# Hybrid encoder layer on one core: the softmax sums spread by DMA, operand transposes in three steps, gate rows woven into a projection

## The chip, the cores and the metric

The kernel runs on one core of a Trainium2 chip. The metric is the device time of one execution in microseconds (us). Before the change it is 1793.68 us, the median of three runs (1793.61 to 1795.17).

The engines are named as in the profile: PE is TensorE (matmuls and transposes; PEld is its weight load, which overlaps), DVE is VectorE, ACT is ScalarE, POOL is GpSimd and SP is the queue that issues the DMAs. Each engine works through its own list of instructions in a fixed order, so an instruction that waits holds up all that stand behind it.

## The reference

One layer (DEPTH is 1) over two sequences, a prompt of 512 tokens and a sample of 2048, each with 16 learned meta tokens in front. D_MODEL is 1024, all in fp32. A projection feeds two head groups; their outputs go through one output projection back into the residual.

```python
def hybrid_layer(h, norm_g, w_in, b_gate, conv_w, mlstm_norm_g, q_norm_g, k_norm_g, rpb, w_out):
    xn = rms_norm(h, norm_g)
    proj = xn @ w_in                                  # 4112 + 512 columns
    q_m, k_m, v_m, o_m, z_m, gates, q_a, k_a, v_a, z_a = jnp.split(proj, cuts, axis=-1)
    qk_m = jax.nn.silu(centred_dwconv(jnp.concatenate([q_m, k_m], axis=-1), conv_w))
    ...
    h_m = mlstm_bidir(heads_m(q_m), heads_m(k_m), heads_m(v_m), gates)   # scans in chunks
    y_m = rms_norm(sigmoid(o_m) * h_m, ...) * silu(z_m)
    qa, ka, va = rms_norm(heads_a(q_a), q_norm_g), rms_norm(heads_a(k_a), k_norm_g), heads_a(v_a)
    y_a = neighbourhood_attention(qa, ka, va, rpb) * silu(z_a)
    return h + jnp.concatenate([y_m, y_a], axis=-1) @ w_out

# neighbourhood_attention: 8 heads of 64; tokens lie on a grid 64 wide; a query sees a window of
# 8 x 16 tokens with a learned bias, and the 16 meta tokens
p = softmax(concat([q . k * scale + bias, q . k_meta * scale]))
out = p_window @ v + p_meta @ v_meta
```

The mLSTM gates give, per direction, cumulative sums and running maxima over each chunk of 128 tokens and from chunk to chunk. These are the "gate rows".

## The kernel before

**Stages.** The sample's first 1280 tokens and the meta tokens are normalised and transposed to the first set of blocks (h1). `phase_a1` projects them to q, k, v of the attention and to the gates, `phase_a1_z` to the attention's gate path z, `phase_a2` to the columns of the mLSTM. Then the same is done for the second set (h2: the rest of the sample, and the prompt): `phase_a1` (its groups 0 to 5), `phase_a1_z`, `phase_a2`. The mLSTM chunks and the output projection come last. Each projection is three matmul passes per weight tile (L239: high and low parts of an fp32 split), into tiles `mmt` (128 tokens x 256 columns) or `mmf` (128 columns x up to 512 tokens).

**Attention beside the projections.** Attention runs in pairs of heads, 8 pairs (two windows of rows) beside the end of the first set and `phase_a1` of the second, 12 pairs (three windows) beside `phase_a1_z` and `phase_a2` of the second. A generator yields after each step, and `weave(main, (att, 0.6), ...)` advances it by so many steps per step of the projection. A pair has four blocks of 128 queries. `scores(b)` makes two `sps` tiles on PE, which DVE reduces to a maximum (L863) and ACT exponentiates with the row sums in `sums` (L864). `probs(b)` transposes the result (`pps`, L876), copied to `pt` by ACT (L880) and DVE (L882). `values(half)` multiplies by v into `py` (L901). `prep(0)` transposes the queries (`qps`, L833), `prep(1)` the keys, eight transposes (`kps`, L839). `out()` takes 1/sum (L911), has POOL spread it over 64 columns (`rx`, L913), PE transpose that four times (`rb`, L916), and DVE multiply z by it (L918) and by `py` (L919).

**Gate rows.** `R.gate_rows(tp)` runs between the second `phase_a1` and the second `phase_a1_z`, after `drain(att)`. It uses buffers of the attention pool (`gmisc` in tag kt, `gbig` in tag vt). Per direction it is a chain through PE (`gps`, `gpr`, `gpc`, `gpt`, `gpd`), DVE scans and small ACT functions.

**What sets the order.** A scheduler places instructions, but the matmuls that go through `turn()` (projections, `sps`, `pps`, `py`, `qps`, `kps`) are tied on PE to the order in which the code emits them. The gate rows and `rb` are not. All DMAs go through SP. PSUM pools have two buffers each: `ps_mm` for the projections, `ps_a` for `sps`, `ps_b` for `pps`, `kps` and the mLSTM's small products, `ps_c` for `qps`, `py`, `rb` and the gate rows.

```python
    weave(R.phase_a2([meta] + h1, ap, free.append), (att, 0.3), (rl, 3))
    weave(R.phase_a1(blocks2, ap), (att, 0.6), (rl, 3))
    drain(att)
    R.last = False
    R.gate_rows(tp)
    zdone = set()
    att = R.attention(tp, [3, 4, 0], zdone)
    R.last = None
    weave(R.phase_a1_z(h2, ap, zdone), (att, 1.2))
```

Of the kernel before, what the change touches and what calls it, by code (L numbers as in the profile page):

```python
# [92 lines left out]
class Run:  # L93
# [4 lines left out]
    def setup(self):  # L98
# [18 lines left out]
        self.one = cp.tile([1, 128], F32, name="one")  # L117
        nc.vector.memset(self.one, 1.0)

        self.gates = cp.tile([128, 4, 21, 4], F32, name="gates")  # L120
# [20 lines left out]
        self.kqs = {"P": d("kqsP", [1024, NM + LP]), "S": d("kqsS", [1024, NM + LS])}  # L141
        self.yas = d("yas", [512, 2560])
        self.Mrow = d("Mrow", [2, 84 * 128])
        self.cbs = d("cbs", [20, 128, 4 * 129])
# [200 lines left out]
    def phase_a1(self, blocks, pool, first=None):  # L345

        nc, a = self.nc, self.a
        g0 = 0
        if first:
            g0 = 2  # L350
            for blk in blocks:
                for gi in range(2):
                    yield from self.a1_unit(pool, gi, self.A1[gi][1], first[gi], blk)
        for gi in range(g0, 6):
            c0, n = self.A1[gi]
            w = self.load_w(a["w_in"], c0, n)
            for blk in blocks() if callable(blocks) else blocks:
                yield from self.a1_unit(pool, gi, n, w, blk)

    def phase_a1_z(self, blocks, pool, done):  # L360
# [119 lines left out]
    def attention(self, pool, wins, zdone):  # L480

        todo = [AttPair(self, pool, wi, pair) for wi in wins for pair in range(4)]
        todo[0].load()
        todo[0].prep(0)
        yield
        todo[0].prep(1)
        yield
        prev = None
        for n, p in enumerate(todo):
            after = todo[n + 1] if n + 1 < len(todo) else None  # L490
            p.start()
# [12 lines left out]
            p.probs(1)  # L504
            if after:
                after.prep(0)
            if prev:
                while prev.pair not in zdone:
                    yield
                prev.out()  # L510
            yield
            p.values(0)
            p.scores(3)
            p.probs(2)
            if after:
                after.prep(1)
            yield
            prev = p
        prev.probs(3)
        yield  # L520
        yield
        prev.values(1)
        while prev.pair not in zdone:
            yield
        yield
        prev.out()


    def gate_rows(self, pool):
        nc = self.nc  # L530
        LNC = math.log(128.0 ** -0.5)
        NR = 84
        cp = self.const
        misc = pool.tile([128, 8, 128], F32, tag="kt", name="gmisc", bufs=2)
        zero, ones = misc[:NR, 0, :], misc[:NR, 1, :]
        nc.vector.memset(zero, 0.0)
        nc.vector.memset(ones, 1.0)
        self.cols = cp.tile([128, 2, 4, NR], F32, name="gcols")
        for d in range(2):
            big = pool.tile([128, 8, 128], F32, tag="vt", name=f"gbig{d}", bufs=2)  # L540
            mn, t, b, a, A, M, ws, ac = (big[:NR, i, :] for i in range(8))
            E = t
            row = misc[0:1, 2 + 3 * d:5 + 3 * d, :].rearrange("p a b -> p (a b)")[:, :4 * NR].rearrange("p (i r) -> p i r", i=4)
            col = self.gcol[:, d, :]
# [10 lines left out]
            nc.vector.tensor_tensor(out=a, in0=ps[:NR, 0:128], in1=b, op=ALU.subtract)  # L555
            nc.vector.tensor_tensor_scan(out=rv(A), data0=rv(a), data1=rv(zero), initial=-BIG, op0=ALU.max, op1=ALU.add)
            last = slice(127, 128) if d == 0 else slice(0, 1)
            bL, AL = b[:, last], A[:, last]
# [9 lines left out]
            for c0, nch in ((0, 4), (4, 16)):  # L568
# [6 lines left out]
                if d == 0:  # L575
                    nc.vector.tensor_copy(out=row[:, 2, fa:fa + 4], in_=row[:, 3, m0])
                    nc.vector.tensor_copy(out=row[:, 2, fa + 4:fb], in_=row[:, 3, fa:fb - 4])
                else:
                    nc.vector.tensor_copy(out=row[:, 2, fa:fb - 4], in_=row[:, 3, fa + 4:fb])
            pc = self.ps_c.tile([128, 512], F32, tag="c", name="gpc")  # L580
            nc.tensor.matmul(pc[:NR, 0:1], row[:, 2, :], self.one[:, 0:1], start=True, stop=True)
# [11 lines left out]
            nc.vector.tensor_scalar(out=M, in0=M, scalar1=mp, scalar2=None, op0=ALU.subtract)  # L593
            nc.sync.dma_start(out=self.Mrow[d].rearrange("(r j) -> r j", r=NR), in_=M)
            pt = self.ps_c.tile([128, 512], F32, tag="c", name="gpt")
            for i, x in enumerate((ac, ws, E)):
# [7 lines left out]
            nc.tensor.matmul(pd[:, 0:NR], self.one, drow, start=True, stop=True)  # L604
            nc.vector.tensor_copy(out=cols[:, 3, :], in_=pd[:, 0:NR])


# [154 lines left out]
    def load_wo(self, pool):  # L762
# [4 lines left out]
        for k in range(8):  # L767
            wr = pool.tile([128, 1024], F32, tag="wor", name="wor", bufs=1)
            nc.sync.dma_start(out=wr, in_=v[:, k, :])
            if k < 4:  # L770
                nc.vector.tensor_scalar(out=wr, in0=wr, scalar1=self.mg[:, k:k + 1], scalar2=None, op0=ALU.mult)
# [30 lines left out]
class AttPair:  # L802
# [9 lines left out]
    def load(self):  # L812
        nc, r, pool, nr, nk, f = self.nc, self.r, self.pool, self.nr, self.nk, self.f
        self.kt = pool.tile([128, 8, 128], F32, tag="kt", name="kt", bufs=2)
        self.vt = pool.tile([128, 8, 128], F32, tag="vt", name="vt", bufs=2)
        self.qt = pool.tile([128, 4, 128], F32, tag="qt", name="qt", bufs=2)
# [8 lines left out]
    def prep(self, part):  # L825

        nc, r, pool, nk = self.nc, self.r, self.pool, self.nk
        if part == 0:
# [6 lines left out]
            return  # L835
        for half in range(2):
            ps = r.ps_b.tile([128, 512], F32, tag="t", name="kps")
            for c in range(4):
                r.turn(nc.tensor.transpose(ps[:, c * nk:(c + 1) * nk], self.kt[:nk, half * 4 + c, :], r.ident[:nk, :nk]))  # L839
            nc.scalar.activation(out=self.K[:, half * 4 * nk:(half + 1) * 4 * nk], in_=ps[:, :4 * nk], func=AF.Copy, scale=r.gk)  # L840

    def start(self):
        pool = self.pool
        self.py = self.r.ps_c.tile([128, 512], F32, tag="c", name="py")
        self.sums = pool.tile([128, 2, 4], F32, tag="sums", name="sums", bufs=2)
        self.bias, self.pts, self.s, self.first = {}, {}, {}, True

    def scores(self, b):
        nc, r, pool, nk, n, bt = self.nc, self.r, self.pool, self.nk, 3 * self.nk, BTYPE[b]
        if bt not in self.bias:  # L850
            self.bias[bt] = pool.tile([128, 2, n], F32, tag="bias", name="bias", bufs=4)
            nc.sync.dma_start(out=self.bias[bt], in_=r.a[f"bias{self.wt}"][self.pair, bt])
# [7 lines left out]
        for hh in range(2):  # L860
            s = pool.tile([128, 384], F32, tag="s", name="s", bufs=6)
            mx = pool.tile([128, 1], F32, tag="mx", name="mx", bufs=4)
# [21 lines left out]
    def values(self, half):  # L884

        nc, r, nk, pts = self.nc, self.r, self.nk, self.pts.pop(half)
        order = ((1, 4, 0, 2, 3), (6, 3, 7, 5, 4))[half]
        for c in order:
# [8 lines left out]
            for run in runs:  # L897
# [4 lines left out]
                self.first = False  # L902

    def out(self):
        nc, r, pool = self.nc, self.r, self.pool
# [3 lines left out]
        zv = view(zt[:, :], [[8, 8], [64, 8], [1, 8]])  # L909

        nc.vector.reciprocal(out=self.sums, in_=self.sums)  # L911
        rx = pool.tile([128, 4, 2, 64], F32, tag="rx", name="rx", bufs=1)
        nc.gpsimd.tensor_scalar(out=rx, in0=view(self.sums[:, 0, 0:1], [[1, 4], [4, 2], [0, 64]]), scalar1=0.5, scalar2=None, op0=ALU.mult)  # L913
# [24 lines left out]
def drain(g):  # L938
    for _ in g:
        pass  # L940
# [3 lines left out]
def hymba(ctx, tc, a):  # L944
# [200 lines left out]
```

## Time and profile before

| | us |
|---|---|
| median of three runs | 1793.68 |
| the profiled execution | 1794.23 |
| its span, first to last instruction | 1792.5 |
| PE busy | 1693.5 (94%) |
| DVE, ACT, POOL busy | 906.5, 683.2, 405.3 |

The stages by the trace: the first blocks and their q, k, v, z until about 225 us, the first `phase_a2` with attention pairs until about 645, the second `phase_a1` until 843.4 (its attention ends near 720), the gate rows until 869, the second `phase_a1_z` and the first part of `phase_a2` with 12 attention pairs until about 1270, the rest of `phase_a2` until 1415, and the mLSTM with the output projection until the end. In the profile, a matmul's record overlaps the next one's, so the spacing of starts is what one costs.

### The profile page before, as it was taken

The numbers are of one execution on the slowest core, as the hardware profiler recorded it, in microseconds if no ns is written. First come the engines' busy times: TensorE is split into PE (matmuls) and PEld (weight loads), VectorE is DVE, ScalarE is ACT, GpSimd is POOL, SyncE is SP. The second block draws the span as 40 slices with busy tenths as digits, with TensorE's granted clock in tenths as the row PEclk, the third lists the DMA queues.
The fourth block names the chain that finished last, engine by engine and source line by source line (L and its number), as shares of the span: only waits on it lengthen the run. The fifth ranks groups of instructions, "written<-read, shape, count | busy, mean of one in ns | idle before, by whom it ended". The sixth has DMA issues, their size and how long they took to land. (4 is left out here: it accounts for less than half of the span.)

```text
span 1792.5 us, 32992 instructions
## 1 busy us (share of the span) xinstructions
PE 1693.5 (94%) x12476; PEld 1501.2 (84%) x12476; DVE 906.5 (51%) x2564; ACT 683.2 (38%) x1715; POOL 405.3 (23%) x383
## 2 busy tenths in 40 slices
PE   6999999999999989999799999999999899999899
PEld 6999988888989978998577777878888888877787
DVE  8896015253361266640334455353464378776662
ACT  5432223343342354222234445444444354543430
POOL 4021122221131231111011212211444232322210
PEclk9999999999999999999799999999999999999999
DMA  5466332333444554332454556754566666555431
GB/s 185 136 218 168 91 102 73 101 98 106 121 123 120 169 174 118 93 97 84 96 151 131 161 147 167 200 163 133 187 184 177 194 206 187 190 182 189 148 129 71
DMA packets 247166, 258.57 MB, mean 144 GB/s; under 512 B 17928, under 2 KB 204624, under 8 KB 247008
## 3 DMA queue, kind: packets, MB, share of 16 engines
q1 hardware_dynamic: 247008, 256.47, 47.7%
q8 instruction: 98, 1.61, 0.4%
q14 instruction: 60, 0.49, 0.1%
HBM read 183.05 MB, written 73.37 MB: 143 GB/s over the span
## 5 line engine op out<-in xcount | busy, mean ns | idle before, releaser
L239 PE MATMUL mmt<-wh,xah 128*128 128x256 f32 (+1 forms) x1536 | 438.9, 286 | 3.4 <-ACT mlo L260 3.4
L239 PE MATMUL mmt<-wl,xah 128*128 128x256 f32 (+1 forms) x1536 | 436.5, 284 | 1.4 <-POOL wl L230 1.4
L239 PE MATMUL mmt<-wh,xal 128*128 128x256 f32 (+1 forms) x1536 | 435.6, 284 | 0.0
L230 POOL TENSOR_TENSOR wl<-wr,wh 128x512 fp32r<-128x512 f32 (+1 forms) x184 | 247.3, 1357 | 700.0 <-ACT wh L229 691.9
L239 PEld LDWEIGHTS mmt<-wh,xah 128*128 128x128 f32 x1536 | 291.3, 190 | 4.7 <-ACT mlo L260 3.8
L239 PEld LDWEIGHTS mmt<-wl,xah 128*128 128x128 f32 x1536 | 290.8, 189 | 2.2 <-POOL wl L230 1.8
L239 PEld LDWEIGHTS mmt<-wh,xal 128*128 128x128 f32 x1536 | 292.3, 190 | 0.4 <-DVE xal L216 0.2
L387 DVE SCALAR_TENSOR_TENSOR acc<-craw,cw,acc 128x256 f32<-128x256 f32 (+2 forms) x192 | 147.1, 766 | 63.4 <-ACT acc L385 58.4
L229 ACT CAST wh<-wr 128x512 fp32r<-128x512 f32 (+1 forms) x184 | 110.1, 621 | 180.9 <-DMA wr<-in_w_in 135.1
L239 PE MATMUL mmf<-xah,wh 128*128 128x512 f32 x384 | 154.0, 401 | 3.0 <-ACT craw L431 1.5
L863 DVE CUSTOM_DVE_ANT_0 s<-sps,bias 128x384 f32<-128x384 f32 (+3 forms) x160 | 71.9, 483 | 161.7 <-PE sps L859 161.1
L239 PE MATMUL mmf<-xal,wh 128*128 128x512 f32 x384 | 152.0, 396 | 0.0
L239 PE MATMUL mmf<-xah,wl 128*128 128x512 f32 x384 | 151.6, 395 | 0.0
L239 PE MATMUL mmt<-wh,xbh 128*128 128x256 f32 (+1 forms) x384 | 112.3, 292 | 4.0 <-ACT xbh L215 2.7
L239 PE MATMUL mmt<-wl,xbh 128*128 128x256 f32 (+1 forms) x384 | 111.0, 289 | 0.0
L239 PE MATMUL mmt<-wh,xbl 128*128 128x256 f32 (+1 forms) x384 | 110.6, 288 | 0.4 <-DVE xbl L216 0.4
L864 ACT ACTIVATE s<-s,mx 128x384 f32<-128x384 f32 (+3 forms) x160 | 88.4, 555 | 22.0 <-DVE mx L863 21.4
L699 POOL TENSOR_TENSOR qw<-qw,kq 128x1024 f32<-128x1024 f32 (+1 forms) x20 | 63.4, 3168 | 131.9 <-ACT qw L698 121.8
L329 ACT COPY raw<-mmt 128x512 f32<-128x512 f32 x50 | 29.3, 585 | 159.1 <-PE mmt L239 152.3
L239 PEld LDWEIGHTS mmf<-xah,wh 128*128 128x128 f32 x384 | 72.6, 189 | 19.6 <-ACT craw L431 2.4
L373 DVE SCALAR_TENSOR_TENSOR zt<-zt,mmf 128x512 f32<-128x512 f32 (+1 forms) x24 | 14.4, 599 | 143.7 <-ACT zt L372 135.3
L239 PEld LDWEIGHTS mmf<-xah,wl 128*128 128x128 f32 x384 | 72.3, 188 | 17.2
(236 smaller groups left out, 3453.9 us busy)
## 6 DMA issues: line engine op xcount, KB each, us to landing
wr<-in_w_in SPq DMA_DIRECT2D x176, 256.0 KB
ozs<-vbuf SPq DMA_DIRECT2D x40, 256.0 KB
X<-Mrow SPq DMA_DIRECT2D x20, 512.0 KB
oz<-ozs SPq DMA_DIRECT2D x20, 512.0 KB
v<-vms SPq DMA_DIRECT2D x38, 256.0 KB
bias<-in_bias SPq DMA_DIRECT2D x24, 384.0 KB
x<-in_xs SPq DMA_DIRECT2D x16, 512.0 KB
kq<-kqsS SPq DMA_DIRECT2D x16, 512.0 KB
```

The source lines that it names most:

```text
L229: nc.scalar.copy(out=wh[:, ks, :n], in_=wr[:, :, :n])
L230: nc.gpsimd.tensor_tensor(out=wl[:, ks, :n], in0=wr[:, :, :n], in1=wh.bitcast(F32)[:, ks, :n], op=ALU.subtract)
L239: self.turn(nc.tensor.matmul(ps, st(s, k), mv(m, k), start=i == 0, stop=i == last))
L329: nc.scalar.copy(out=raw, in_=ps)
L373: nc.vector.scalar_tensor_tensor(out=t[:, :n], in0=t[:, :n], scalar=1.0, in1=ps[:, :n], op0=ALU.add, op1=ALU.mult)
L387: nc.vector.scalar_tensor_tensor(out=acc[:, :n], in0=raw[:, d:d + n], scalar=self.cw[:, ct, d:d + 1], in1=acc[:, :n], op0=ALU.mult, op1=AL ...
L699: nc.gpsimd.tensor_tensor(out=qw[:, :nd], in0=qw[:, :nd], in1=qT.unsqueeze(1).to_broadcast([128, nd, 4, 128]), op=ALU.mult)
L863: nc.vector.tensor_tensor_reduce(out=s[:, :n], in0=pss[hh][:, :n], in1=self.bias[bt][:, hh], op0=ALU.add, op1=ALU.min, scale=-1.0, scalar= ...
L864: nc.scalar.activation(out=s[:, :n], in_=s[:, :n], func=AF.Exp, scale=-1.0, bias=mx[:, 0:1], accum_out=self.sums[:, hh, b:b + 1])
```

## The change

Four things, and two smaller ones.

1. `out()` loses `rx` and the four `rb` transposes. A new step `weights()` takes 1/sum, writes it to a DRAM scratch (`rsum`, 2 x 4 x 128), and reads it back as two broadcasts over 64 partitions each into an SBUF tile `rb`. The factor 0.5 that `rx` held moves to the rows 4 to 7 of w_out in `load_wo`.
2. `prep` has three parts: queries, four key transposes, four key transposes. The key tiles go from pool `ps_b` to `ps_c`, and `py` is allocated at the first `values`, not at `start`.
3. `gate_rows` becomes a generator, on buffers of the pool `bp`. It waits until the gates are projected (`gated`) and attention has ended (`rested`), and is woven into the second `phase_a1` at 0.25 steps per step.
4. `load()` is called two pairs ahead, with three `vt` buffers. To pay for it, `bias` goes from 4 to 3 buffers and `s` from 6 to 4.

```diff
-        todo[0].load()
-        todo[0].prep(0)
-        yield
-        todo[0].prep(1)
-        yield
+        for i in range(3):
+            todo[0].prep(i)
+            yield
+        todo[1].load()
...
             p.scores(0)
             if prev:
                 prev.probs(3)
-            if after:
-                after.load()
             yield
             if prev:
                 prev.values(1)
             p.scores(1)
             p.probs(0)
+            if prev:
+                prev.weights()
+            if after:
+                after.prep(0)
             yield
             p.scores(2)
             p.probs(1)
             if after:
-                after.prep(0)
+                after.prep(1)
...
                 prev.out()
+            if n + 2 < len(todo):
+                todo[n + 2].load()
             yield
             p.values(0)
             p.scores(3)
             p.probs(2)
             if after:
-                after.prep(1)
+                after.prep(2)
...
     def gate_rows(self, pool):
+        while self.gated < 2 or not self.rested:
+            yield
...
-            if k < 4:
-                nc.vector.tensor_scalar(out=wr, in0=wr, scalar1=self.mg[:, k:k + 1], ...)
+            nc.vector.tensor_scalar(out=wr, in0=wr, scalar1=self.mg[:, k:k + 1] if k < 4 else 0.5, ...)
...
+    def weights(self):
+        nc.vector.reciprocal(out=self.sums, in_=self.sums)
+        rows = r.rsum[r.nsum % 2]
+        r.nsum += 1
+        nc.sync.dma_start(out=rows.rearrange("h b q -> q h b"), in_=self.sums)
+        self.rb = self.pool.tile([128, 512], F32, tag="rb", name="rb", bufs=1)
+        for hh in range(2):
+            nc.sync.dma_start(out=self.rb[hh * 64:hh * 64 + 64], in_=bcast(rows[hh].rearrange("b q -> (b q)"), 64))
...
-        nc.gpsimd.tensor_scalar(out=rx, ...)
-        rb = r.ps_c.tile([128, 512], F32, tag="c", name="rb")
-        for b in range(4):
-            nc.tensor.transpose(rb[:, b * 128:(b + 1) * 128], rx[:, b].rearrange("p h d -> p (h d)"), r.ident)
-        nc.vector.tensor_tensor(out=zv, in0=pv(rb), in1=zv, op=ALU.mult)
+        nc.vector.tensor_tensor(out=zv, in0=pv(self.rb), in1=zv, op=ALU.mult)
...
-    weave(R.phase_a1(blocks2, ap), (att, 0.6), (rl, 3))
+    gates = R.gate_rows(bp)
+    weave(R.phase_a1(blocks2, ap), (att, 0.6), (rl, 3), (gates, 0.25))
     drain(att)
+    drain(gates)
     R.last = False
-    R.gate_rows(tp)
```

**PE, the gate rows.** Before, both directions stand in one piece between the first column tile of z (`mmf`) and the second attention's query transposes (`qps`):

```order
L239 MATMUL mmf<-xbh,wl 128x256
L560 MATMUL gpr<-ident,gbig_9869 1x84
L561 MATMUL gpr<-ident,gbig_9869 1x84
L581 MATMUL gpc<-one,gmisc 84x1
L582 MATMUL gpc<-one,gmisc 84x1
L597 MATMUL gpt<-ident,gbig_9869 128x84 x3
L598 MATMUL gpt<-ident,gcol 1x84
L604 MATMUL gpd<-gmisc,one 128x84
L547 MATMUL gps<-ident,gates 84x128
```

Now each piece stands between projection matmuls (`mmt`) of the second `phase_a1`; this is the piece `gpt` of the first direction:

```order
L245 MATMUL mmt<-wl,xah 128x256
L245 MATMUL mmt<-wh,xal 128x256
L614 MATMUL gpt<-ident,v_8652 128x84 x2
L614 MATMUL gpt<-ident,kT 128x84
L615 MATMUL gpt<-ident,gcol 1x84
L245 MATMUL mmt<-wh,xah 128x256
L245 MATMUL mmt<-wl,xah 128x256
```

Between one piece and the next of a direction now stand 25 or more matmuls of the projection, where before there were none.

**DVE, 1/sum and its use.** These are the rows around the second pair's reciprocal in the second attention; `ISA s,mx` is the reduction of `scores`, `pt` the copy of `probs`. Before:

```order
L882 COPY pt<-pps 128x3x128
L911 RECIPROCAL sums<-sums 128x8
L373 SCALAR_TENSOR_TENSOR zt<-zt,mmf 128x256
L863 ISA s,mx<-sps,bias 128x384
L863 ISA mx 128x1
```

Now:

```order
L898 COPY pt<-pps 128x3x128
L925 RECIPROCAL sums<-sums 128x8
L940 TENSOR_TENSOR zt<-rb,zt 128x8x8x8
L381 SCALAR_TENSOR_TENSOR zt<-zt,mmf 128x512
L879 ISA s,mx<-sps,bias 128x384
L879 ISA mx 128x1
```

The multiplication by `rb` (L940), which waits for the broadcast DMAs, stands right behind the reciprocal here and ahead of the next reductions; behind the other reciprocals stand up to two blocks' reductions before it.

**SP, the new DMAs.** The same pair on SP; `rsum` is the write of 1/sum, `rb` its broadcasts, `vt`, `kt` the loads ahead:

```order
L837 DMA kt<-ks 96x8x128
L838 DMA kt<-kmeta 8x8x128
L928 DMA rsum_109<-sums 128x8x1
L931 DMA rb<-rsum_109 64x512 x2
L383 DMA zs<-zt 128x512
L868 DMA bias<-in_bias 128x768
L837 DMA vt<-vs 96x8x128
```

The broadcasts stand directly behind the write that they wait for, with z's stores, a bias table and the next loads behind them on the queue.

## Rows read from the trace of the kernel before

**Rows 1.** The page: busy times, PE and its granted clock in 40 slices
```profile
PE 1693.5 (94%) x12476; PEld 1501.2 (84%) x12476; DVE 906.5 (51%) x2564; ACT 683.2 (38%) x1715; POOL 405.3 (23%) x383
PE   6999999999999989999799999999999899999899
PEclk9999999999999999999799999999999999999999
```
**Rows 2.** Stretches: us, busy PE, PEld, DVE, ACT, POOL, granted clock, DMA share, GB/s
```profile
846.80:869.40 22.60, 6.65 (x26) 3.89 (x26) 13.31 (x58) 8.31 (x16) 3.19 (x3) 0.62 0.35 97
870.20:877.20 7.00, 7.00 (x29) 5.62 (x28) 0.75 (x1) 0.06 (x1) 0.00 (x0) 0.83 1.02 181
```
**Rows 3.** PE in order of time, 846 to 874: start, us, instruction
```profile
846.36 0.28 PE L239 MATMUL mmf<-xbl,wh 128*128 128x256 f32 x1
846.47 0.28 PE L239 MATMUL mmf<-xbh,wl 128*128 128x256 f32 x1
848.16 0.23 PE L560 MATMUL gpr<-ident,gbig 84*1 84x84 f32 x1 [1.41 <-DVE gbig L554]
...
869.42 1.11 PE L833 MATMUL qps<-ident,qt 128*128 128x128 f32 x4
```
**Rows 4.** Groups of PE from 846.8 to 869.4, costliest first: idle before, releasers
```profile
L581 PE MATMUL gpc<-one,gmisc 1*84 1x1 f32 x4 | 0.9, 282 | 6.0 <-DVE gmisc L577 4.3 <-DVE gmisc L579 1.6
L560 PE MATMUL gpr<-ident,gbig 84*1 84x84 f32 x2 | 0.5, 267 | 4.8 <-DVE gbig L554 4.8
```
**Rows 5.** PE in order of time, one pair's `rb` and `py`
```profile
990.77 0.28 PE L239 MATMUL mmt<-wl,xbh 128*128 128x256 f32 x1
990.89 0.28 PE L239 MATMUL mmt<-wh,xbl 128*128 128x256 f32 x1
991.01 0.60 PE L916 MATMUL rb<-ident,rx 128*128 128x128 f32 x4
992.70 0.44 PE L901 MATMUL py<-pt,vt 128*64 128x128 f32 x4 [1.08 <-DVE zt L918]
```
**Rows 6.** Instructions on tile `rb`: ns min/median/max
```profile
L916 PE MATMUL rb<-ident,rx x80: 270/273/329, 415.1 to 1270.5; 128*128 128x128 f32 x80
```
**Rows 7.** Waits of PE over the whole span: us, times, longest
```profile
PE kps L839 <- ACT pt L880: 8.6, 18, 2.7
PE kps L839 <- DVE pt L882: 7.6, 5, 2.6
PE py L901 <- DVE zt L918: 5.8, 7, 1.1
PE sps L859 <- ACT K L840: 2.1, 1, 2.1
```
**Rows 8.** Stretches around the longest waits of `kps`, columns as in Rows 2
```profile
645.00:652.00 7.00, 2.31 (x10) 1.92 (x11) 6.86 (x15) 4.90 (x12) 4.37 (x4) 0.66 0.60 197
652.00:660.00 8.00, 8.00 (x59) 7.25 (x58) 3.57 (x15) 2.43 (x7) 2.44 (x2) 0.87 0.27 85
907.00:918.00 11.00, 9.27 (x78) 7.69 (x79) 3.13 (x12) 5.32 (x14) 4.01 (x3) 0.84 0.89 217
998.00:1006.00 8.00, 8.00 (x56) 7.81 (x60) 0.20 (x1) 1.91 (x5) 1.63 (x2) 0.79 0.66 201
```
**Rows 9.** Issue times on SP by line, ns min/median/max; reciprocal on DVE; key copy on ACT
```profile
L594 SPq DMA_DIRECT2D Mrow<-gbig x2: 325/343/361, 856.4 to 867.4; - x2
L154 SPq DMA_DIRECT2D mg<-in_mlstm_norm_g x1: 1897/1897/1897, 6.2 to 6.2; - x1
L820 SPq DMA_DIRECT2D kt<-ks x20: 316/382/607, 148.8 to 1156.8; - x20
L911 DVE RECIPROCAL sums<-sums x20: 196/203/204, 372.7 to 1253.2; 128x8 f32<-128x8 f32 x20
L840 ACT ACTIVATE K<-kps,gk x40: 478/591/692, 310.9 to 1226.6; 128x512 f32<-128x512 f32 x16, 128x384 f32<-128x384 f32 x8, 128x416 f32<-128x416 f32 x8, 128x288 f32<-128x288 f32 x8
```
**Rows 10.** Waits of SP over the whole span
```profile
SPq L228 <- POOL wl L230: 168.8, 107, 6.6
SPq L820 <- DMA Mrow<-gbig: 2.3, 2, 1.1
```
**Rows 11.** All engines in order of time: a load of two DMAs and its first use
```profile
846.93 0.97 SPq L228 DMA_DIRECT2D wr<-in_w_in  x2
...
849.73 0.62 ACT L229 CAST wh<-wr 128x512 fp32r<-128x512 f32 x1 [0.79 <-DMA wr<-in_w_in]
```
**Rows 12.** PE in order of time: block 3, the next pair's block 0, values
```profile
994.06 0.88 PE L859 MATMUL sps<-K,Q 64*64 64x384 f32 x8
...
1005.74 0.76 PE L859 MATMUL sps<-K,Q 64*64 64x312 f32 x8
...
1010.07 0.44 PE L901 MATMUL py<-pt,vt 128*64 128x128 f32 x4
```

More of the change, by code (lines that the diff above doesn't have):

```diff
@@ L118, in setup @@
         nc.vector.memset(self.one, 1.0)
+        self.zo = cp.tile([128, 2, 128], F32, name="zo")
+        nc.vector.memset(self.zo[:, 0, :], 0.0)
+        nc.vector.memset(self.zo[:, 1, :], 1.0)
+        self.gated, self.rested = 0, False
         self.gates = cp.tile([128, 4, 21, 4], F32, name="gates")
@@ L142, in setup @@
         self.yas = d("yas", [512, 2560])
+        self.rsum = [d(f"rsum{i}", [2, 4, 128]) for i in range(2)]
+        self.nsum = 0
         self.Mrow = d("Mrow", [2, 84 * 128])
@@ L353, in phase_a1 @@
                     yield from self.a1_unit(pool, gi, self.A1[gi][1], first[gi], blk)
+            self.gated += 1
         for gi in range(g0, 6):
@@ L358, in phase_a1 @@
                 yield from self.a1_unit(pool, gi, n, w, blk)
+            self.gated += gi == 0
     def phase_a1_z(self, blocks, pool, done):
@@ L520, in attention @@
         yield
+        prev.weights()
         yield
@@ L526, in attention @@
         prev.out()
+        self.rested = True
     def gate_rows(self, pool):
@@ L533, in gate_rows @@
         cp = self.const
[L534 to L537, printed above, removed]
+        while self.gated < 2 or not self.rested:
+            yield
+        zero, ones = self.zo[:NR, 0, :], self.zo[:NR, 1, :]
         self.cols = cp.tile([128, 2, 4, NR], F32, name="gcols")
         for d in range(2):
-            big = pool.tile([128, 8, 128], F32, tag="vt", name=f"gbig{d}", bufs=2)
-            mn, t, b, a, A, M, ws, ac = (big[:NR, i, :] for i in range(8))
+            big = [pool.tile([128, 4, 128], t) for t in ("kT", "v1")]
+            mn, t, b, a, A, M, ws, ac = (x[:NR, i, :] for x in big for i in range(4))
+            rowt = pool.tile([128, 4, 128], "kw")
             E = t
-            row = misc[0:1, 2 + 3 * d:5 + 3 * d, :].rearrange("p a b -> p (a b)")[:, :4 * NR].rearrange("p (i r) -> p i r", i=4)
+            row = rowt[0:1, :, :].rearrange("p a b -> p (a b)")[:, :4 * NR].rearrange("p (i r) -> p i r", i=4)
             col = self.gcol[:, d, :]
@@ L605, in gate_rows @@
             nc.vector.tensor_copy(out=cols[:, 3, :], in_=pd[:, 0:NR])
+            yield
     def load_k(self, pool, seq, col0, n):
@@ L769, in load_wo @@
             nc.sync.dma_start(out=wr, in_=v[:, k, :])
-            if k < 4:
-                nc.vector.tensor_scalar(out=wr, in0=wr, scalar1=self.mg[:, k:k + 1], scalar2=None, op0=ALU.mult)
+            nc.vector.tensor_scalar(out=wr, in0=wr, scalar1=self.mg[:, k:k + 1] if k < 4 else 0.5, scalar2=None, op0=ALU.mult)
             nc.scalar.copy(out=self.woh[:, k, :], in_=wr)
@@ L814, in load @@
         self.kt = pool.tile([128, 8, 128], F32, tag="kt", name="kt", bufs=2)
-        self.vt = pool.tile([128, 8, 128], F32, tag="vt", name="vt", bufs=2)
+        self.vt = pool.tile([128, 8, 128], F32, tag="vt", name="vt", bufs=3)
         self.qt = pool.tile([128, 4, 128], F32, tag="qt", name="qt", bufs=2)
@@ L835, in prep @@
             return
[L836 to L840, printed above, removed]
+        half = part - 1
+        ps = r.ps_c.tile([128, 512], F32, tag="c", name="kps")
+        for c in range(4):
+            r.turn(nc.tensor.transpose(ps[:, c * nk:(c + 1) * nk], self.kt[:nk, half * 4 + c, :], r.ident[:nk, :nk]))
+        nc.scalar.activation(out=self.K[:, half * 4 * nk:(half + 1) * 4 * nk], in_=ps[:, :4 * nk], func=AF.Copy, scale=r.gk)
     def start(self):
         pool = self.pool
-        self.py = self.r.ps_c.tile([128, 512], F32, tag="c", name="py")
         self.sums = pool.tile([128, 2, 4], F32, tag="sums", name="sums", bufs=2)
@@ L850, in scores @@
         if bt not in self.bias:
-            self.bias[bt] = pool.tile([128, 2, n], F32, tag="bias", name="bias", bufs=4)
+            self.bias[bt] = pool.tile([128, 2, n], F32, tag="bias", name="bias", bufs=3)
             nc.sync.dma_start(out=self.bias[bt], in_=r.a[f"bias{self.wt}"][self.pair, bt])
@@ L860, in scores @@
         for hh in range(2):
-            s = pool.tile([128, 384], F32, tag="s", name="s", bufs=6)
+            s = pool.tile([128, 384], F32, tag="s", name="s", bufs=4)
             mx = pool.tile([128, 1], F32, tag="mx", name="mx", bufs=4)
@@ L886, in values @@
         nc, r, nk, pts = self.nc, self.r, self.nk, self.pts.pop(half)
+        if self.first:
+            self.py = r.ps_c.tile([128, 512], F32, tag="c", name="py")
         order = ((1, 4, 0, 2, 3), (6, 3, 7, 5, 4))[half]
@@ L909, in out @@
         zv = view(zt[:, :], [[8, 8], [64, 8], [1, 8]])
-        nc.vector.reciprocal(out=self.sums, in_=self.sums)
-        rx = pool.tile([128, 4, 2, 64], F32, tag="rx", name="rx", bufs=1)
-        nc.gpsimd.tensor_scalar(out=rx, in0=view(self.sums[:, 0, 0:1], [[1, 4], [4, 2], [0, 64]]), scalar1=0.5, scalar2=None, op0=ALU.mult)
-        rb = r.ps_c.tile([128, 512], F32, tag="c", name="rb")
-        for b in range(4):
-            nc.tensor.transpose(rb[:, b * 128:(b + 1) * 128], rx[:, b].rearrange("p h d -> p (h d)"), r.ident)
         pv = lambda t: view(t[:, :], [[64, 8], [8, 8], [1, 8]])
-        nc.vector.tensor_tensor(out=zv, in0=pv(rb), in1=zv, op=ALU.mult)
+        nc.vector.tensor_tensor(out=zv, in0=pv(self.rb), in1=zv, op=ALU.mult)
         nc.vector.tensor_tensor(out=zv, in0=pv(self.py), in1=zv, op=ALU.mult)
```

4 lines of the change are left out of this document (added).

## The prediction

> **What bounds the kernel now.** I read the page first: PE is busy 94% of the span and its row of 40 slices shows 9 almost everywhere [rows 1]. So only two things can move the time much: PE work that goes, and the few places where PE stands still or runs at the lower of its two clock levels. One slice stands out, the twentieth, with PE at 7 and the granted clock at 7 [rows 1]. The table of stretches shows it as 846.8 to 869.4 us: 22.6 us in which PE is busy 6.65 us, DVE 13.31 and the clock is granted at 0.62, a mixture of 2.4 and 1.2 GHz; the next 7 us run at 0.83 [rows 2]. PE's timeline shows what stands there: the last matmul of z's first column tile starts at 846.47, the second attention's first query transposes at 869.42, and between them are only the gate rows [rows 3]; the groups of that stretch show PE waiting for DVE's small operations [rows 4]. The reader is to see that this piece is a chain with nothing beside it.
>
> Next I read PE's waits over the whole span. Three kinds belong to attention: `kps` for the copies of `pt`, 8.6 and 7.6 us (both share pool `ps_b`), `py` for DVE's first multiplication in `out()`, 5.8 us, and `sps` once for the key copy, 2.1 us [rows 7]. The stretches around the longest of them show the clock at 0.66 to 0.87 [rows 8].
>
> **The change part by part.**
>
> *Gate rows.* From the start of the last z matmul to the start of `qps` is 869.42 - 846.47 = 22.95 us, of which that matmul takes 0.11 [rows 3]: 22.8 us. The gate matmuls remain: 26 records [rows 2], charged at 0.11 us each, what a transpose of 128 columns costs below: 2.9 us. The four `qps` take 1.11 us here against 0.60 for four like ones at full clock [rows 3, 5], 0.5 to gain, and 7.0 us at 0.83 means that (1 - 0.83) / 0.5 = 34% of it ran at half clock, which costs half of that, 1.2 us [rows 2]. Sum: 22.8 - 2.9 + 0.5 + 1.2 = 21.6 us. The cover is the second `phase_a1`, in which PE runs without a gap after its attention ends. PE is bound to its order, so a gate matmul whose DVE input is late stops the projection, but 25 or more matmuls of 0.12 us stand between the pieces, 3 us at least, against 4.3 us for the longest wait on one releaser in rows 4. If the cover fails wholly, the 10.8 us of waits in rows 4 come back.
>
> *`rb`.* 80 transposes go [rows 6]. Four make a record of 0.60 us; records overlap the next by 0.28 - 0.12 = 0.16 us, as the projection's rows show (starts 0.12 apart, 0.28 long) [rows 5]. So 0.44 us a pair, times 20: 8.8 us. Behind them `py` waited for DVE's multiplication by `rb`, 5.8 us in 7 places [rows 7]; with `rb` in SBUF and `py` in its own slot that goes: 5.8 us. POOL's `rx` goes too, which PE never waited for: nothing.
>
> *Transposes in three steps.* `kps` leaves pool `ps_b`, so it no longer waits for `pt`: 8.6 + 7.6 + 2.1 = 18.3 us [rows 7]. I don't credit all. Between 645 and 652, where the two longest waits of `kps` stand, DVE is busy 6.86 of 7 us [rows 8]; what is late there is DVE itself, and the next `pps` would meet the same backlog. Half of those two waits (2.7 and 2.6) stays: 18.3 - 2.6 = 15.7 us. What is late next is `ps_c`, where four tiles a pair share two buffers in place of three. The nearest row is the key copy, 0.59 us [rows 9]: `py` or the second `kps` can wait that long for it. Bounds 0 to 0.6 us a pair, below nothing excluded since the waits removed are counted already; I take 0.2, 4 us in all.
>
> *Clock.* The three lower stretches of rows 8 that follow such waits lose (1 - granted clock) times their length: 1.0, 1.8 and 1.7 us. If the waits go, so does this. I credit 3 of 4.5.
>
> *The new chain.* The trace of before has neither a store of 1024 single elements nor its broadcasts. From below: a store like `Mrow`, issued in 0.34 us, after which the next DMA waited 1.1 us [rows 9, 10]; then two loads, from first issue to first use 849.73 - 846.93 = 2.8 us [rows 11]; with the reciprocal 0.2 us: 4.4 us. From above: `mg`, 512 single elements, took 1.90 us to issue [rows 9]; twice that is 3.8 us in place of 0.34: 7.9 us. I take the upper, since `mg` is the row nearest in shape. The room: block 3's scores start at 994.06, the next block's at 1005.74, and `py`, which needs the last probabilities, at 1010.07 [rows 12]. Taking off 2.5 us for PE, DVE and ACT before the reciprocal can start, and the 1.7 us of waits and 1.7 of clock that lie in this cycle [rows 7, 8], the next reductions come 11.7 - 2.5 - 3.4 = 5.8 us behind the reciprocal, `py` 10.1. Queued behind L940 on DVE are the next reductions and the copy to `pt`, and for those `pps`, `py` and PE wait. So where L940 stands directly behind the reciprocal DVE is late by at most 7.9 - 5.8 = 2.1 us, and `py` still has 2 us. Bounds 0 to 2.1 us for the 12 later pairs (the 8 earlier ones have steps of twice the length); I take 0.5: 6 us.
>
> The Trainium skill ("DMA: Bandwidth & Descriptors", Rules for kernel authors) says that a DMA whose last dimension is strided becomes one descriptor per element, and advises a contiguous last dimension. `mg` against `kt` agrees as far as rows 9 go: 512 single elements cost 1.90 us to issue, 960 runs of 512 B 0.38. Were the rule of no weight here, the chain would be the lower one and the sum 6 us better.
>
> *SP.* Each pair adds 0.34 to 3.8 us of issue, the wait for landing, and two issues of 0.48 [rows 9 to 11], up to 5.9 us. SP mostly waits for producers: 168.8 us for POOL's weight parts alone [rows 10]. So I charge nothing; without that slack it is the slower rival below.
>
> *Loads two pairs ahead, fewer `bias` and `s` buffers.* PE's list shows no wait for `kt`, `vt`, `qt` or `bias` worth a row, so nothing is gained; a `bias` that is late would stop DVE and is in the range. The four extra multiplications in `load_wo` lie beside DVE's idle time: nothing.
>
> Sum: 21.6 + 8.8 + 5.8 + 15.7 + 3.0 - 4 - 6 = 44.9 us. The profiled execution took 1794.23 us, half a microsecond above the median of three, so 1794.2 - 44.9 = 1749 us.
>
> **The rivals.**
>
> *The waits of `kps` only move.* `ps_c` is fuller than before, and ACT and DVE, the late ones, do the same work. Against it: `kps` comes in two halves a step apart. Then 15.7 and 3.0 stay: 1749 + 18.7 = 1768 us.
>
> *DVE stands behind the broadcast.* For it: L940 is at its place in DVE's order whatever the DMAs do, and SP is in order too. Against it: the room above. If it costs 3 us at each of the 12 later pairs in place of 0.5: 1749 + 30 = 1779 us.
>
> *The gate rows are not covered*, so that the change doesn't do what it says there: the 10.8 us of waits return: 1760 us.
>
> *SP becomes the bound, slower than before.* The place is SP's list between `rsum` and `rb`: up to 5.9 us a pair, 118 us in all, in which weights, tables and loads behind it stand still. It decides from 45 / 20 = 2.2 us a pair reaching PE. If half of 118 reaches it in place of what I charged: 1749 - 6 + 59 = 1802 us. The skill's rule on strided elements above is what would drive it. For it: one queue for all DMAs; against it: the slack in rows 10, and that no load of attention shows among PE's waits.
>
> **How the numbers follow.** Forecast 0.60, moved waits 0.18, DVE behind the broadcast 0.10, gates not covered 0.05, SP 0.07. The range's lower end is all credits in full with no new cost: 1749 - 10 - 4 = 1735 us. The upper end reaches past the moved waits towards DVE's rival: 1775 us. A change of 0.2%, 3.6 us, is about what can be told from none. Only the SP rival is slower, and a mixture of the rivals might end near none: faster 0.91, same 0.03, slower 0.06.
>
> **What would show it.** Right: no stretch of 20 us with the clock near 0.6 between the second `phase_a1` and z; no `rb` on PE; waits of `kps` under 5 us in all; waits of PE for `rb`'s multiplication small. Wrong: a long wait of DVE for a DMA at L940 with `pps` or `py` waiting for DVE behind it; `py` or `kps` waiting for the key copy or for L941 for over 10 us in all; weights (L234) that PE waits for; an issue time of `rsum` over 3.8 us.

## The result: 5.45% slower

The changed kernel takes 1891.22 us (median of 4 runs, 1890.20 to 1894.32) against 1793.64 before on the same chip: ratio 1.0545, interval 1.0527 to 1.0563. It was forecast 45 us faster and came out 98 us slower.

The page after, the rows that answer to [rows 1]: busy time, share and instructions, then tenths in 40 slices.

```profile
PE 1713.4 (91%) x12396; PEld 1518.9 (80%) x12396; DVE 906.1 (48%) x2568; ACT 680.8 (36%) x1715; POOL 379.1 (20%) x363
PE   6999999989989978999978868887888989998999
PEclk9999999999989989999989989998889999999999
```

PE has 80 instructions fewer and is busy 20 us longer, while more of its work ran at the lower clock level (mean granted clock 0.957 against 0.983); and it is idle 1888.6 - 1713.4 = 175 us, against 99 before. No slice stands at 7 with the clock at 7 any more. These are the times of [rows 2] and [rows 3] in the trace after (us, PE, PEld, DVE, ACT, POOL busy, granted clock, DMA share, GB/s). The work in them isn't the same: the projection of `phase_a1` runs here with the second direction's gate rows between its matmuls, from `gpr` at 846.2 to the last `gpd` at 873.3.

```profile
846.00:874.00 28.00, 28.00 (x237) 27.60 (x236) 3.55 (x23) 7.08 (x13) 5.20 (x5) 1.00 0.53 135
```

So the woven gate rows leave PE no gap and no lower clock, as forecast, and the loss is elsewhere. From the starts of the first and last `sps`, `py` and `ops` rows in PE's timeline of each trace (the last column is the experiment with 1/sum by transposes, below):

```
us                              before   after   transposes
first attention, sps to py       403.4   442.7     386.6
from there to the second's py    171.5   149.6     151.2
second attention, py to py       363.7   432.9     350.4
from there to the first ops      168.9   171.5     164.6
```

The loss is mostly inside the two attentions: 39 and 69 us against before, 56 and 83 against the third column, which is 7.0 us a pair in the first attention and 6.9 in the second. The waits after say how (us in all, times, longest). DVE first:

```profile
DVE zt L940 <- DMA rb<-rsum: 212.6, 18, 15.0
```

PE, in place of [rows 7], has no wait of `kps` left, but two new ones for DVE:

```profile
PE py L919 <- DVE pt L898: 56.7, 9, 11.9
PE sps L875 <- DVE mx L879: 32.6, 6, 8.6
```

And SP, beside [rows 10]:

```profile
SPq L931 <- DMA rsum<-sums: 162.7, 20, 9.5
```

That is 8.1 us at each of the 20 pairs, where `Mrow`'s store made the next DMA wait 1.1. One pair shows the whole chain. DVE's list, with its idle time before a row in brackets:

```profile
961.82 0.20 DVE L925 RECIPROCAL sums<-sums 128x8 f32<-128x8 f32 x1 [0.67 <-ACT s L880]
975.40 0.69 DVE L940 TENSOR_TENSOR zt<-rb,zt 128x512 f32<-128x512 f32 x1 [13.38 <-DMA rb<-rsum]
976.01 0.68 DVE L381 SCALAR_TENSOR_TENSOR zt<-zt,mmf 128x512 f32<-128x512 f32 x1
976.61 0.55 DVE L879 CUSTOM_DVE_ANT_0 s<-sps,bias 128x384 f32<-128x384 f32 x1
...
977.57 0.55 DVE L898 COPY pt<-pps 128x384 f32<-128x384 f32 x1
```

SP's and PE's of the same time:

```profile
962.38 0.39 SPq L928 DMA_DIRECT2D rsum<-sums  x1
970.88 1.12 SPq L931 DMA_DIRECT2D rb<-rsum  x2
```

```profile
968.26 0.43 PE L919 MATMUL py<-pt,vt 128*64 128x128 f32 x2 [0.24 <-ACT pt L896]
978.17 2.61 PE L919 MATMUL py<-pt,vt 128*64 128x128 f32 x22 [9.47 <-DVE pt L898]
```

The reciprocal starts at 961.82. The store's issue starts at 962.38 and takes 0.39 us; it has landed at 970.88, 8.5 us after that start. The broadcasts take 4.5 more. L940, which the order has directly behind the reciprocal, starts 13.6 us after it; over the 20 pairs that time is 12.8 to 19.0 us. Behind it on DVE stand the reduction and the copy to `pt`, and PE waits 9.47 us for that copy. What the DMA engines did meanwhile (columns as above):

```profile
964.40:966.40 2.00, 2.00 (x13) 1.37 (x12) 0.00 (x0) 0.00 (x0) 0.00 (x0) 1.00 0.72 78
966.40:968.40 2.00, 1.76 (x16) 0.92 (x16) 0.00 (x0) 1.08 (x2) 0.00 (x0) 1.00 0.00 0
968.40:970.90 2.50, 0.30 (x2) 0.06 (x1) 0.00 (x0) 0.00 (x0) 0.00 (x0) 1.00 0.00 0
970.90:975.40 4.50, 0.00 (x0) 0.00 (x0) 0.00 (x0) 0.00 (x0) 0.00 (x0) 0.71 0.21 58
```

From 966.4 to 970.9 the trace shows them moving nothing: no packet is under way and the store is still not complete, while SP, next in line for `rb`, issues no other load. Then DVE, ACT and PE stand together and the granted clock falls: 0.71 is a mixture of 2.4 and 1.2 GHz.

### The profile page after: what moved, and what is told of

It is laid out like the page before. It is cut to its first block, busy times and chain, and to the rows that moved or that the text cites. A ratio compares the mean times of both kernels' runs of the same rounds, so it can differ in the third digit from the quotient of the medians.

```text
span 1888.6 us, 32950 instructions
## 1 busy us (share of the span) xinstructions
PE 1713.4 (91%) x12396; PEld 1518.9 (80%) x12396; DVE 906.1 (48%) x2568; ACT 680.8 (36%) x1715; POOL 379.1 (20%) x363
## 5 line engine op out<-in xcount | busy, mean ns | idle before, releaser
L245 PE MATMUL mmt<-wh,xah 128*128 128x256 f32 (+1 forms) x1536 | 444.2, 289 | 16.4 <-DVE vbuf L480 5.7
L245 PEld LDWEIGHTS mmt<-wh,xah 128*128 128x128 f32 x1536 | 295.4, 192 | 19.7 <-DVE vbuf L480 6.1
L245 PEld LDWEIGHTS mmt<-wl,xah 128*128 128x128 f32 x1536 | 295.1, 192 | 1.8 <-POOL wl L236 1.0
L245 PEld LDWEIGHTS mmt<-wh,xal 128*128 128x128 f32 x1536 | 296.2, 193 | 0.5 <-DVE xal L222 0.2
L395 DVE SCALAR_TENSOR_TENSOR acc<-craw,cw,acc 128x256 f32<-128x256 f32 (+2 forms) x192 | 153.4, 799 | 63.8 <-ACT acc L393 60.2
L919 PE MATMUL py<-pt,vt 128*64 128x128 f32 (+11 forms) x960 | 73.5, 297 | 57.0 <-DVE pt L898 56.7
L940 DVE TENSOR_TENSOR zt<-rb,zt 128x512 f32<-128x512 f32 x20 | 13.8, 692 | 222.9 <-DMA rb<-rsum 212.6
L919 PEld LDWEIGHTS py<-pt,vt 128*64 128x64 f32 (+3 forms) x960 | 56.7, 153 | 69.9 <-DVE pt L898 58.8
L875 PE MATMUL sps<-K,Q 64*64 64x384 f32 (+3 forms) x640 | 69.9, 493 | 32.6 <-DVE mx L879 32.6
```

The source lines that it names most:

```text
L245: self.turn(nc.tensor.matmul(ps, st(s, k), mv(m, k), start=i == 0, stop=i == last))
L395: nc.vector.scalar_tensor_tensor(out=acc[:, :n], in0=raw[:, d:d + n], scalar=self.cw[:, ct, d:d + 1], in1=acc[:, :n], op0=ALU.mult, op1=AL ...
L875: r.turn(nc.tensor.matmul(pss[hh][qp, :n], self.Q[hp, b * 128 + half * 64:b * 128 + half * 64 + 64], self.K[hp, k0:k0 + n], start=True, st ...
L919: r.turn(nc.tensor.matmul(self.py[hh * 64:(hh + 1) * 64, g * 64:(g + len(run)) * 64], self.vt[:nk, c, hh * 64:(hh + 1) * 64], mv, start=se ...
```

## Experiments

Theory A: DVE stands at L940 until `rb` has landed and holds PE. Theory B: SP stands between `rsum` and `rb`, and what it would have issued comes late. Theory C: the other three parts cost the time. Each ratio is to the kernel before on the same chip; differences of ratios are turned into us by 1794. By their intervals such a difference is good to some 5 to 10 us.

**Undo one part, do one alone.** First, the changed kernel with `rx` and `rb` as before:

```diff
-        prev.weights()
+        rx = pool.tile(...); nc.gpsimd.tensor_scalar(out=rx, in0=<sums, spread>, scalar1=1.0, ...)
+        for b in range(4):
+            nc.tensor.transpose(rb[:, b * 128:(b + 1) * 128], rx[:, b]..., r.ident)
```

> The changed kernel with 1/sum spread as before (rx on POOL, four rb transposes on PE, rb in PSUM); gate rows woven, transposes in three steps, loads two ahead and the smaller buffers stay. Theory A (DVE stands at L940 until the broadcast has landed, and holds reductions, evictions and PE behind it): 1794 - (21.6 + 15.7 + 3.0 - 4) = 1758 us, and no wait of DVE for a DMA at the multiplication by rb. Theory B (SP is held between rsum and rb, so loads and weights behind it are late): 1758 us as well. Theory C (the other three parts cost the time: three ps_c tiles more, fewer bias and s buffers): stays within 15 us of 1891 us.

1749.24 us, ratio 0.9741 [0.9720, 0.9762]. Theory C falls: the spread alone costs 0.080 x 1794 = 144 us. Its page: PE idle 68 us.

```profile
PE 1676.0 (96%) x12476; PEld 1495.3 (86%) x12476; DVE 903.0 (52%) x2568; ACT 681.8 (39%) x1715; POOL 410.2 (24%) x383
```

The other way round, the kernel before with the spread alone:

```diff
+            if prev:
+                prev.weights()
...
-        nc.vector.tensor_tensor(out=zv, in0=pv(rb), in1=zv, op=ALU.mult)
+        nc.vector.tensor_tensor(out=zv, in0=pv(self.rb), in1=zv, op=ALU.mult)
```

> The kernel before with only the spread of 1/sum by DMA. Theory A and B: the changed kernel lost about 1891 - 1758 = 133 us by the spread, so 1794 + 120 to 135 = 1914 to 1929 us, with waits of DVE at the multiplication by rb of some 10 us each in 15 or more pairs. Theory C: near 1794 - 8.8 = 1785 us.

1935.76 us, 1.0779 [1.0757, 1.0801]: 140 us lost, a little over the range. The spread's cost hardly depends on the other parts.

The first of these two with the gate rows back between the attentions:

```diff
-    weave(R.phase_a1(blocks2, ap), (att, 0.6), (rl, 3), (gates, 0.25))
+    weave(R.phase_a1(blocks2, ap), (att, 0.6), (rl, 3))
...
-    drain(gates)
...
+    R.gate_rows(tp)
```

> The run with 1/sum by transposes (1749 us) with the gate rows put back between the two attentions. If the gate rows were worth what the prediction's term says, 1749 + 21.6 = 1771 us, with a stretch of some 22 us at a granted clock near 0.6 before the second attention. If other work had filled the gap or the woven rows cost PE waits elsewhere, under 1760.

1773.42 us, 0.9851 [0.9817, 0.9884]. The woven gate rows are worth 0.0110 x 1794 = 20 us. The old chain is back:

```profile
847.33 0.44 PE L591 MATMUL gpc<-one,gmisc 1*84 1x1 f32 x2 [4.28 <-DVE gmisc L587]
```

**A or B.** `zt` by `py` first, then by `rb`:

```diff
+        nc.vector.tensor_tensor(out=zv, in0=pv(self.py), in1=zv, op=ALU.mult)
         nc.vector.tensor_tensor(out=zv, in0=pv(self.rb), in1=zv, op=ALU.mult)
-        nc.vector.tensor_tensor(out=zv, in0=pv(self.py), in1=zv, op=ALU.mult)
```

> The changed kernel with the two multiplications of out() in the other order, both still on DVE: zt by py first, then by rb. DVE's order now has the multiplication by rb right behind the one by py, half a step or more later than in the changed kernel; SP's list of rsum and rb is the same. Theory A: the broadcast lands 15 to 17 us behind the reciprocal and the multiplication by py comes about 10 us behind it in the later 12 pairs (later still in the first 8), so 5 to 7 us of DVE's wait stay in 12 pairs and py is free in time: 1758 + 12 x 3 = about 1795 us. Theory B: SP's list is unchanged, so within 15 us of 1891 us.

And as this, with the multiplication by `rb` on POOL:

```diff
-        nc.vector.tensor_tensor(out=zv, in0=pv(self.rb), in1=zv, op=ALU.mult)
+        nc.gpsimd.tensor_tensor(out=zv, in0=pv(self.rb), in1=zv, op=ALU.mult)
```

> As the swapped order, but the last multiplication, by rb, is on POOL, for which only the store of zt waits; SP's list still holds the wait for rsum. Theory A: DVE waits for no DMA any more, all credits but a few us come: 1745 to 1760 us. Theory B: SP still stands about 8 us at each rb, so within 15 us of 1891 us, with waits of PE for weights or of DVE for bias. A mixture would show as a time between, with PE waiting for loads.

1835.53 us, 1.0219 [1.0202, 1.0237], and 1831.26, 1.0213 [1.0169, 1.0257]. Neither theory alone: 60 us come back, 85 stay. The swap left DVE 87.4 us of waits for `rb`, POOL's version none. The times agree, but not because DVE's wait is free at its new place: the next reductions stand behind it there as well, and PE waits for them. In the swap, then in the version on POOL:

```profile
PE sps L875 <- DVE mx L879: 39.0, 14, 6.5
```

```profile
PE sps L875 <- DVE mx L879: 9.0, 4, 3.3
```

One place of the swap, DVE's row and PE's:

```profile
1092.47 0.69 DVE L941 TENSOR_TENSOR zt<-rb,zt 128x512 f32<-128x512 f32 x1 [9.34 <-DMA rb<-rsum]
```

```profile
1093.62 1.72 PE L875 MATMUL sps<-K,Q 64*64 64x312 f32 x8 [6.47 <-DVE mx L879]
```

The version on POOL loses about as much elsewhere: PE's waits before `ups`, a product of the mLSTM's, are 28.2 us there against 14.4 in the swap (summed over what ended them). What else makes the two equal was not tested, so the swap shows only part of DVE's hold. SP's wait stays in both; in the version on POOL:

```profile
SPq L931 <- DMA rsum<-sums: 164.1, 18, 10.9
```

**The store, and SP's wait, each by itself.** The transposes' run with the store as well, which nothing reads; then also two loads of half of it, into a tile that nothing uses:

```diff
+        nc.sync.dma_start(out=rows.rearrange("h b q -> q h b"), in_=self.sums)
+        un = pool.tile([128, 256], F32, tag="un", name="un", bufs=1)          # second run only
+        for hh in range(2):
+            nc.sync.dma_start(out=un[hh * 64:hh * 64 + 64], in_=bcast(rows[hh, 0:2]..., 64))
```

> The run with 1/sum by transposes (1749 us), and beside it the store of 1024 single elements at each pair, which nothing reads or waits for. If the store's packets themselves hold the queues or the memory for others, slower than 1749 by 10 us or more; if only waiting for it costs, 1749 within 6 us.

> As the last, and SP also issues two loads of the stored row (half of it, to fit) into a tile that nothing uses: no engine but SP waits for the store. Theory B's share alone: SP stands some 8 us at each pair; if that costs what the run on POOL had left over (1831 - 1749 = 82 us), the time is 1810 to 1840 us, with PE waiting behind late loads; if SP's slack covers it, 1749 to 1765 us, and the 82 us have another cause.

1787.43 us, 0.9933 [0.9906, 0.9961], and 1816.11, 1.0099 [1.0068, 1.0130]. So the store alone costs 34 us, and SP's wait with the loads behind it 30 more. Theory B as I had put it was half of its own share: before SP waits for anything, stores behind this one complete late. ACT waits for `ct`, a tile of the mLSTM's convolution, to be stored before it may write there again; with transposes alone, and with the unread store:

```profile
ACT acc L393 <- DMA kqsS<-ct: 0.2, 1, 0.2
```

```profile
ACT acc L393 <- DMA kqsS<-ct: 26.1, 7, 6.9
```

How much of the 34 us comes by such late stores is not shown. The rest of the 144 us is what lies between this run and the changed kernel: 80 us, which hold DVE's wait, but also full loads, a store one step earlier and four transposes fewer. The version on POOL, which has no wait of DVE for `rb`, still stands 20 us above the run with unused loads; those 20 were not taken apart.

**Move the hold.** The version on POOL, with `rb`'s loads from POOL's queue:

```diff
-            nc.sync.dma_start(out=self.rb[hh * 64:hh * 64 + 64], in_=...)
+            nc.gpsimd.dma_start(out=self.rb[hh * 64:hh * 64 + 64], in_=...)
```

> The run with the last multiplication on POOL (1831 us), with rb's two loads issued from POOL's queue in place of SP's; the store of the sums stays on SP and is as slow to land. Theory B for what was left there (SP held about 8 us at each rb, so that the loads and tables behind it come late): SP waits for rsum no longer, and 1831 - 70 = 1750 to 1775 us. If the hold only moves to POOL and the weight parts behind it come late: 1800 to 1840 us with waits of PE for wl. If neither queue matters: 1831 within 10.

1853.35 us, 1.0298 [1.0260, 1.0335]: worse by 0.0085. That is above each of the times that I had named. POOL now stands for the store, longer than SP did:

```profile
POOL rb L931 <- DMA rsum<-sums: 274.6, 16, 30.5
```

POOL's weight parts stand behind that in its order, but PE shows no wait for `wl`, so how the hold reaches the time here is not shown.

**Why the store lands late.** Same bytes, other shapes. In the changed kernel, 128 runs of 32 bytes (first edit; `rb` then holds the factors in another order, so this run serves for its time alone), or the sums turned by one transpose and stored as 8 runs of 512 bytes (second):

```diff
-        nc.sync.dma_start(out=rows.rearrange("h b q -> q h b"), in_=self.sums)
+        nc.sync.dma_start(out=<rows as 128 runs of 8>, in_=self.sums.rearrange("p h b -> p (h b)"))
...
-        nc.sync.dma_start(out=rows.rearrange("h b q -> q h b"), in_=self.sums)
+        nc.tensor.transpose(ps[:8, 0:128], self.sums.rearrange("p h b -> p (h b)"), r.ident)
+        nc.scalar.copy(out=st, in_=ps[:8, 0:128])
+        nc.sync.dma_start(out=rows.rearrange("h b q -> (h b) q"), in_=st)
```

> The changed kernel with the store of 1/sum as 128 runs of 8 elements, one run a partition, in place of 1024 single elements (as many bytes; so rb holds the factors in another order: which factor a query gets is left wrong, nothing else). If the late landing of the store comes from its single elements, SP's wait for rsum falls from 8.1 us to 1 to 3 us each, the chain from the reciprocal to L940 from 15 to 17 us to 8 to 11, and the time by about half of the 142 us that the spread cost: 1800 to 1840 us. If any store takes that long to land, SP's wait stays at 8 us and the time within 15 us of 1891.

> The changed kernel with the sums transposed once on PE (128x8 to 8x128), copied by ACT and stored as 8 runs of 512 bytes; L940 and L941 as in the changed kernel. If the single elements are the cause, the store lands within 1 to 3 us, the chain is 0.2 + 1 + 2 + 3 to 5 = 6 to 8 us as the prediction had it, and the time 1750 to 1790 us. If the round trip itself is the cause, over 1850 us.

1765.73 us, 0.9805 [0.9778, 0.9833], and 1764.66, 0.9795 [0.9761, 0.9829]. The first came 34 us under its range, the second inside it: once the store lands early, nearly all of the cost goes (133 and 135 of 144 us). Then, in the run with unused loads, 512 single elements, 512 runs of 8 bytes (`rows` as [4, 128, 2]), and 1024 single elements 64 bytes apart (`rows` as [2, 4, 128, 16]):

```diff
+        nc.sync.dma_start(out=rows[0:1].rearrange("h b q -> q h b"), in_=self.sums[:, 0:1, :])
...
+        nc.sync.dma_start(out=rows.rearrange("c q x -> q c x"), in_=<sums in pairs>)
...
+        nc.sync.dma_start(out=rows[:, :, :, 0].rearrange("h b q -> q h b"), in_=self.sums)
```

> As the last, with 512 single elements stored in place of 1024 (only the first head's), the loads as many as there. If the landing grows with the number of single elements, SP's wait for rsum falls from 8 to 4 to 5 us each, and the excess over 1749 us by about half or more; if it is a fixed price of single elements, nothing changes.

> The run with unused loads, with the sums stored as 512 runs of 8 bytes. With 1024 runs of 4 bytes SP waited 9 us, with 512 of 4 bytes 8.3, with 128 of 32 bytes 2.4. If what counts is how many pieces share a stretch of memory, about half: 4 to 5 us, and a time of 1790 to 1800 us. If anything short of a longer run is equally dear, 8 us and 1800 to 1816.

> The run with unused loads (1816 us), with each of the 1024 single elements stored 64 bytes from the next instead of side by side (16 times the span of addresses, as many elements; the two loads behind fetch one element a partition only). If the landing is late because neighbours of 4 bytes fall into the same short stretch of memory, SP's wait for rsum falls from 9 us to 1 to 4. If a single element is dear as such, SP's wait stays at 8 us or more.

1799.46 us, 1.0000 [0.9981, 1.0019]; 1762.67, 0.9790 [0.9768, 0.9813]; 1755.19, 0.9753 [0.9729, 0.9777] (with smaller loads). The pairs came 27 us under their range. SP's waits: 1024 single elements side by side, 512 of them, 512 pairs, 1024 single elements 64 bytes apart, each from its own run:

```profile
SPq L930 <- DMA rsum<-sums: 176.2, 19, 10.9
```

```profile
SPq L930 <- DMA rsum<-sums: 166.3, 20, 10.1
```

```profile
SPq L930 <- DMA rsum<-sums: 80.6, 19, 6.3
```

```profile
SPq L930 <- DMA rsum<-sums: 59.0, 20, 5.0
```

And 128 runs of 32 bytes, and 8 of 512:

```profile
SPq L931 <- DMA rsum<-sums: 42.8, 18, 4.8
```

```profile
SPq L935 <- DMA rsum<-st: 21.4, 17, 2.5
```

Per wait: 9.3, 8.3, 4.2, 2.95, 2.4 and 1.3 us; the last two are from the changed kernel, where 1024 side by side took 8.1. Half the elements change the wait little, though the time falls by 18 of 64 us, which neither of my forecasts had. The same number of elements 64 bytes apart takes off two thirds of the wait, and that run is only 2 us above the transposes. So it is not mainly the count that is dear, nor the packets of so many elements on the DMA engines, but how many separate pieces fall into one short stretch of memory: 16 pieces in 64 bytes (the first two), 8, 1, 2. The count may not be free either: 1024 pieces, one in 64 bytes, wait longer than 128, two in 64 bytes. That 64 is the length that counts was not tried; elements 64 bytes apart also lie over 16 times the addresses.

**A version with a short chain.** The edits of the turned sums and of the swap together, both multiplications on DVE; the same with that by `rb` on POOL; and beside the last one, on one chip, the transposes' run again:

> The run with the sums transposed once (1765 us), with the multiplication by py first and that by rb behind it, both on DVE. Its DVE waited 64 us for rb, 3 us a pair; behind py's multiplication rb has landed. If that wait is what lies between it and the transposes' run, 1735 to 1750 us; if the slot of ps_c that the turned sums take (PE's qps waited 11.9 us for their copy) is the rest, 1750 to 1760 us.

> The run with the sums turned and py multiplied first (1747 us), with the multiplication by rb on POOL. DVE there waited 37 us for rb in 14 pairs, with PE busy 96%: if those waits still reach PE, 1735 to 1743 us; if not, 1747 within 5.

> The run with 1/sum by transposes again, beside the last one on the same chip, to rank the two: 1749 us within 5.

1747.06 us, 0.9716 [0.9686, 0.9746]; 1745.32, 0.9697 [0.9672, 0.9722]; 1752.05, 0.9733 [0.9711, 0.9756]. The one on POOL has the lowest median, 3% below the kernel before and 6.7 us below the transposes on the same chip, with intervals that overlap at the edge. The 37 us that DVE still waited for `rb` in the first of the three gave little when they went; there PE waited for the reductions 0.5 us in all.

## Why the prediction was wrong

**The step that failed is "the new chain".** Its upper bound was 7.9 us, against 13.6 in the pair shown and 12.8 at the least. I built it from two rows of other transfers: how long `mg` takes to issue, and how long the next DMA waited behind `Mrow` [rows 9, 10]. The issue price went the other way (0.37 us for 1024 elements, under `mg`'s 1.90 for 512), the landing, which I had taken from runs of 512 bytes, was 8.1 us in place of 1.1, and the two broadcasts, priced at 2.8 us by [rows 11], took 4.5. `mg` is a load, and no row of before had a store of short pieces, so its landing had no upper bound; I wrote one all the same, and the range rested on it. My own sign of being wrong, a long wait of DVE at L940 with `py` behind it, is what the trace shows. The Trainium skill ("DMA: Bandwidth & Descriptors", Anatomy of one DMA — SWDGE (gpsimd) path) says of DMAs on that path that the semaphore can't rise until the last byte is confirmed in the target memory. This store went by SP; its 4.5 us without a packet are in line with that. The rule that I weighed, one descriptor per strided element, named the right transfer, but the number of descriptors is not what cost here: 1024 of them landed in 2.95 us.

**The room was too small, and not only in the later pairs.** I had 5.8 us for the next reductions and 10.1 for `py`; in the pair shown `py` starts 6.4 us behind the reciprocal. A chain of 13.6 us overruns either, and PE's 32.6 and 56.7 us of waits stand at just these two places. The 8 earlier pairs I had charged nothing, because their steps are twice as long. Against the transposes they lost 7.0 us each, as much as the later ones (SP's part is in both).

**The rivals.** "DVE stands behind the broadcast" named the mechanism and was priced at 3 us in 12 pairs, 36 in all; 60 us came back by the swap, which leaves part of the hold, and the 80 of the last step hold other things too, so its own size is known only as somewhere near these. "SP becomes the bound", the only slower one, came from the right queue by the wrong way: 1802 us was to come from issue times, and what came was 30 us by the wait for the landing and 34 by the store alone, which I had not thought of. I gave each alone; they came together, on one cause. "I charge nothing" for SP was the second failed line.

**What held.** Gate rows: 21.6 forecast; 171.5 - 149.6 = 21.9 us from the stage table, 20 by the experiment (give or take 7). Waits of `kps`: gone, and no `ps_c` wait came in their place. That part with its clock, forecast 15.7 + 3.0 - 4 = 14.7, measured (1 - 0.9851) x 1794 = 27 us (interval 21 to 33) with the loads ahead and the buffers in it: more than I credited. `rb`: forecast 8.8 + 5.8 = 14.6 for no transposes at all; between the last two runs, where one of four stays, it is 6.5 us, hardly resolved. The credits without the charges were 54.9 us, and the best version, where the chain is short, is 0.0303 x 1794 = 54 us below the kernel before. That the sum agrees so well is in part luck: one part gave more than its credit and another less.

## What to carry to other kernels

Price a small DMA by its landing, not its issue, and from a row of the same direction, piece length and spacing; where no row has that, leave the upper end open. Before a value is sent round through memory in order to spread it, turn it on chip so that it leaves in long runs, and put what needs it behind what does not in the engine's order. An operation that waits for a DMA costs what stands behind it in its engine's order: behind DVE's 87 us of waits in the swap PE waited 39 us at `sps`, behind the 37 us with the turned sums 0.5.

## What the runs showed of the hardware

A store of 4 KB in single elements side by side issues in 0.37 us and lands some 8 us later, in the pair shown with 4.5 us in which no packet moves; 64 bytes apart the same elements land in 3. Where nothing waits for it, it still costs 34 us in 20 pairs, and ACT's waits for another store to complete rise from 0.2 to 26.1 us. The Trainium skill (the same page, Specifications) says that pieces under 512 bytes are read, changed and written back; no run here shows the reading back itself. Runs of 4 bytes are under that both side by side and 64 bytes apart, and SP waits 9.3 us for the first and 2.95 for the second, so here the crowding decides, and not the length alone.
